# A log-sum-exp kernel on one core: whole loads until two tiles before the end, stores in rows of unequal counts, the last batch written in four parts

## The chip, the cores and the metric

The kernel runs on one core of a Trainium2 chip. The metric is device time in microseconds (us), lower is better. The profile's span is about 1.9 us shorter than that time (339.2 against 341.11 in the profiled run before), because it counts from the first to the last instruction.

The five engines are TensorE (PE), VectorE (DVE), ScalarE (ACT), GpSimd (POOL) and SyncE (SP), which here only issues DMAs. Sixteen DMA engines move the data.

## The reference

```python
B, S, D, H = 8, 2048, 2048, 8        # x: B x S x D, bias: H x 256, all float32
x_heads = x.reshape(B, S, H, 256).transpose(0, 2, 1, 3) + bias[None, :, None, :]
x_tiled = np.repeat(x_heads, 2, axis=2)
out = log(sum(exp(x_tiled)))         # over the last axis, with the usual maximum
```

134 MB are read and 1 MB is written. Each of the 16,384 rows of x gives eight sums of 256 exponentials, and each logarithm is written twice side by side.

## The kernel before

There are 64 tiles of 256 rows (2 MB: 128 partitions, two rows of 8 KB each). Tiles are counted from 0 to 63. In each tile TensorE adds the bias of heads 0 and 1 into PSUM, and ScalarE takes their exponentials with the sum; for the other six heads ScalarE takes exponentials in place and VectorE multiplies by exp(bias) and sums (twelve multiply-and-sum instructions a tile). Eight tiles make a batch; two tiles later its sums are transposed, ScalarE takes the logarithm, and 128 KB are stored. The parts that matter:

```python
NBUF = 9                                  # buffers of one tile
LAST_CUTS = [[0, 1024, 2048], [0, 512, 1024, 1536, 1792, 2048]]
def pieces(t):                            # how the load and the work of tile t are cut
    left = T - 1 - t
    if left > 8:
        return [(0, K, 0, D)]             # whole, K = 2 rows a partition
    if left > 3:
        return [(k, k + 1, 0, D) for k in range(K)]          # halves: tiles 55 to 59
    cuts = [[0, D // 2, D]] * K if left else LAST_CUTS       # quarters: 60 to 62
    ...
def finish(b, src, n_blk, k_rows, base, i, engines):
    ...                                   # transpose, logarithm (ScalarE) into res[i]
    parts = [(0, H)] if n_blk * n in (n, 2 * S) else [(h, h + 1) for h in range(H)]
    ...                                   # one store of 64 rows of 2 KB for a whole batch
for t in range(T):
    ...                                   # the work of tile t, piece by piece
    if t + NBUF < T:
        load(t + NBUF)
    fb, at = divmod(t - 2, NBLK)
    if fb >= 0 and at == NBLK - 1:
        finish(fb, ..., [nc.sync])        # batches 0 to 6, two tiles late
for k in range(K):                        # tile 63 by itself; tiles 56 to 62 were finished
    finish(B - 1, lambda _: Rz[:, k], 1, 1, S - (K - k) * P, k, [nc.sync])   # within it
```

The softmax here doesn't subtract the row's maximum and nothing guards it: scores larger than these inputs give would overflow.

## Time and profile before

The time before is 341.08 us (median of 3, 340.43 to 341.75). The page of the profile, cut. The two rows of slices cut the span in 40: the busy share of the DMA engines in tenths, and the rate in GB/s. The line below them is the share of the chain of waits by engine.

```profile
span 339.2 us, 3449 instructions
PE 238.3 (70%) x408; PEld 70.3 (21%) x408; DVE 271.8 (80%) x1538; ACT 295.0 (87%) x609; POOL 6.3 (2%) x14
...
DMA  8999999999999999999999999999999999988950
GB/s 300 427 433 428 424 429 430 429 429 426 425 430 430 423 427 424 436 423 428 425 435 417 431 425 428 430 428 425 429 432 424 428 418 420 422 346 277 309 209 19
...
q14 instruction: 20, 0.16, 0.1%
...
DMA 75%; ACT 17%; PE 4%; POOL 1%; issue 1%; DVE 0%; POOLq 0%; DVEq 0%; SPq 0%; ACTq 0%
```

ScalarE is busy for 87%, but the chain is DMA for 75%. The chain in order of time shows why: start, duration, what. A tile costs ScalarE 4.44 us (from one exponential of a whole tile, 2.65 us, to the next) as long as data lies ready. Then it has caught up, and the chain jumps to loads.

```profile
20.81 2.65 ACT xt L164
23.46 0.40 ACT ps L156 x2
23.88 0.87 ACT ps L156 x4
24.77 0.47 ACT ps L156 x2
25.25 2.65 ACT xt L164
...
58.93 35.23 DMA xt<-in_x_dram
```

SyncE's timeline (start, duration, what, count; a row covers all issues of a kind in a row) shows one store a batch, and the waits of its queue (total us, times, longest us) show what it waits for. In this kernel a DMA is issued only when the DMA eight before it has landed (the first line), so eight are in flight; a load also waits until VectorE has freed its buffer (the second).

```profile
58.93 4.76 SPq L90 DMA_DIRECT2D xt<-in_x_dram  x2
63.89 0.55 SPq L214 DMA_DIRECT2D out_dram<-res  x1
68.81 32.94 SPq L90 DMA_DIRECT2D xt<-in_x_dram  x8
105.27 0.47 SPq L214 DMA_DIRECT2D out_dram<-res  x1
```

```profile
SPq L90 <- DMA xt<-in_x_dram: 153.3, 59, 5.4
SPq L90 <- DVE R L170: 111.5, 51, 7.5
SPq L214 <- DMA xt<-in_x_dram: 16.5, 7, 3.5
```

The fall of the rate at the end of the page, from 422 to 277 GB/s, looks like bandwidth that small packets lose. It is not. The trace also records when each of the sixteen DMA engines marks a DMA as done. Counted from it, this is how far the others are ahead of the last one:

```
load (from 1)  landed (last mark)   second-last engine ahead by   first engine ahead by
     4             23.31                     0.2 us                     1.0 us
    24            124.78                     2.0 us                     4.3 us
    44            227.46                     5.7 us                     8.3 us
    55            283.58                     7.0 us                    10.3 us
```

One engine falls behind. It takes 4.89 us for its share of a load, like the others, but about every 25.7 us a load takes it 5.86 us. At each of those steps an 8 KB packet of instruction fetch (queue 14 of the page) lies in the trace: it takes 0.325 us, and the 16 KB packet after it 1.273 us in place of 0.61 us, 0.98 us together, close to the step of 0.97 us. (The packets carry no engine's number; that these fetches run on the late engine is what run e7 below shows.) At 300 us the other engines have run out of issued work, which thins the rate; the late one goes on at full speed. A load counts as landed only when the late one is done, so **the late engine's sum of work sets the time**. After the last landing (331.62 us) come another 7.57 us of arithmetic and stores.

The last lines of ScalarE before; "L199" is a logarithm, a bracket is idle time and its releaser:

```profile
332.72 0.58 ACT L199 ACTIVATE res<-tps 56x512 f32<-56x512 f32 x1
333.20 1.75 ACT L164 ACTIVATE xt<-xt 128x512 f32<-128x512 f32 x4
334.85 0.36 ACT L199 ACTIVATE res<-tps 8x256 f32<-8x256 f32 x1
336.48 0.37 ACT L199 ACTIVATE res<-tps 8x256 f32<-8x256 f32 x1 [1.28 <-PE tps L186]
```

ScalarE ends its last exponential at 334.95, 3.3 us after the last landing: at the end the arithmetic lags behind the loads.

### The profile page before, as it was taken

What the parts mean: (1) busy time and instruction counts of PE and PEld (TensorE: products, weight loads), DVE (VectorE), ACT (ScalarE), POOL (GpSimd) and SP (SyncE); (2) the same over time, 40 slices, a digit from 0 to 9 for tenths busy, and PEclk for the clock granted to TensorE, in tenths of its full rate; (3) what the DMA queues carried; (4) which work ended last, traced back from release to release, by engine and by line L of the source; (5) the groups of instructions that cost most, each with busy time, mean ns of one, the idle gap of its engine ahead of it and who ended that gap; (6) DMA issues with size and microseconds to landing.
All of it is one profiled execution on the core that took longest, in us unless ns stands there. A gap on an engine that the chain in (4) does not pass through costs nothing.

```text
span 339.2 us, 3449 instructions
## 1 busy us (share of the span) xinstructions
PE 238.3 (70%) x408; PEld 70.3 (21%) x408; DVE 271.8 (80%) x1538; ACT 295.0 (87%) x609; POOL 6.3 (2%) x14
## 2 busy tenths in 40 slices
PE   5296985866785966776965765766766667868791
PEld 2031222221121221221221221221221212212120
DVE  0429999998887887887898798797798788998775
ACT  2379999998997997988998898898899899998895
POOL 6100000000000000000000000000000000000000
PEclk9999577587876587876589877698777698595756
DMA  8999999999999999999999999999999999988950
GB/s 300 427 433 428 424 429 430 429 429 426 425 430 430 423 427 424 436 423 428 425 435 417 431 425 428 430 428 425 429 432 424 428 418 420 422 346 277 309 209 19
DMA packets 12921, 135.50 MB, mean 399 GB/s; under 512 B 1625, under 2 KB 1897, under 8 KB 4577
## 3 DMA queue, kind: packets, MB, share of 16 engines
q1 hardware_dynamic: 12800, 135.27, 95.6%
q14 instruction: 20, 0.16, 0.1%
q8 instruction: 3, 0.05, 0.1%
q10 hardware_dynamic: 2, 0.01, 0.0%
q0 software_dynamic: 96, 0.00, 0.0%
HBM read 134.23 MB, written 1.05 MB: 399 GB/s over the span
## 4 chain that ended last, share of the span: by engine, by line
DMA 75%; ACT 17%; PE 4%; POOL 1%; issue 1%; DVE 0%; POOLq 0%; DVEq 0%; SPq 0%; ACTq 0%
DMA xt<-in_x_dram 72%; ACT xt L164 10%; ACT ps L156 6%; PE ps L150 3%; DMA b<-bparts 2%; DMA brow<-in_bias_dram 1%; PE ps L145 1%; ACT res L199 0%; DVE junk L170 0%; POOL brest L117 0%; POOL brest L119 0%; POOL bparts L116 0%; POOL bparts L118 0%; POOL b L122 0%; POOL bparts L120 0%
## 5 line engine op out<-in xcount | busy, mean ns | idle before, releaser
L170 DVE CUSTOM_DVE_ANT_0 junk<-xt,w_rep 128x256 f32<-128x256 f32 x768 | 271.0, 420 | 63.4 <-ACT xt L164 63.2
L150 PE MATMUL ps<-xt,ident 128*128 128x512 f32 x256 | 188.8, 872 | 84.0 <-DMA xt<-in_x_dram 83.5
L164 ACT ACTIVATE xt<-xt 128x3072 f32<-128x3072 f32 (+4 forms) x83 | 179.4, 2172 | 20.0 <-DMA xt<-in_x_dram 17.2
L156 ACT ACTIVATE ps<-ps 128x256 f32<-128x256 f32 x256 | 94.6, 370 | 14.0 <-PE ps L150 9.2
L150 PEld LDWEIGHTS ps<-xt,ident 128*128 128x128 f32 x256 | 58.0, 254 | 164.5 <-DMA xt<-in_x_dram 119.5
L170 DVE DVE_READ_ACCUMULATOR2_ANT R<- 128x1 f32 x756 | 61.9, 82 | 0.0
L145 PE MATMUL ps<-b,ones 3*128 3x512 bf16 x128 | 47.0, 439 | 6.5 <-DMA b<-bparts 6.5
L156 ACT ACTIVATION_READ_ACCUMULATOR ps<-ps 128x1 f32 x256 | 48.7, 190 | 0.0
L145 PEld LDWEIGHTS <-ones 3*128 3x128 bf16 x128 | 7.9, 95 | 83.1 <-issue 75.1
L126 PE MATMUL ps<-brow,ones 1*128 1x512 f32 x6 | 5.5, 1078 | 3.6 <-DMA brow<-in_bias_dram 3.6
L133 ACT ACTIVATE w_rep<-ps 128x512 f32<-128x512 f32 x3 | 1.8, 597 | 5.9 <-PE ps L126 5.9
L199 ACT ACTIVATE res<-tps 64x512 f32<-64x512 f32 (+2 forms) x10 | 5.3, 535 | 1.3 <-PE tps L186 1.3
L186 PEld LDWEIGHTS tps<-ident,R 128*64 128x64 f32 (+1 forms) x16 | 2.4, 150 | 7.9 <-ACT ps L156 5.0
L186 PE MATMUL tps<-ident,Rz 128*8 128x128 f32 x2 | 0.7, 374 | 4.1 <-DVE Rz L170 4.1
L186 PE MATMUL tps<-ident,R 128*64 128x128 f32 (+1 forms) x16 | 3.6, 317 | 0.0
L126 PEld LDWEIGHTS ps<-brow,ones 1*128 1x128 f32 x6 | 1.8, 323 | 5.6 <-issue 5.6
L100 ACT ACT_TABLE_LOAD x1 | 1.3, 1283 | 0.7 <-PEq L279 0.7
L122 POOL DMA_DIRECT2D b<-bparts x3 | 1.6, 540 | 0.0
L117 POOL TENSOR_TENSOR brest<-brow,bparts 1x512 f32<-1x512 f32 x1 | 1.1, 1143 | 0.1
L119 POOL TENSOR_TENSOR brest<-brest,bparts 1x512 f32<-1x512 f32 x1 | 1.1, 1142 | 0.1
L186 PEld LDWEIGHTS tps<-ident,Rz 128*8 128x8 f32 x2 | 0.2, 83 | 4.7 <-DVE Rz L170 2.4
L170 DVE DVE_READ_ACCUMULATOR2_ANT Rz<- 128x1 f32 x12 | 1.0, 83 | 0.0
(11 smaller groups left out, 3.0 us busy)
## 6 DMA issues: line engine op xcount, KB each, us to landing
xt<-in_x_dram SPq DMA_DIRECT2D x55, 2048.0 KB
xt<-in_x_dram SPq DMA_DIRECT2D x10, 1024.0 KB
xt<-in_x_dram SPq DMA_DIRECT2D x14, 512.0 KB
out_dram<-res SPq DMA_DIRECT2D x7, 128.0 KB
xt<-in_x_dram SPq DMA_DIRECT2D x3, 256.0 KB
xt<-in_x_dram SPq DMA_DIRECT2D x2, 128.0 KB
out_dram<-res SPq DMA_DIRECT2D x8, 14.0 KB
b<-bparts POOLq DMA_DIRECT2D x3, 1.0 KB, 5.6
```

Source lines behind the costliest of these rows:

```text
L100: nc.scalar.add_instruction(mybir.InstLoadActFuncSet(name=nc.get_next_instruction_name(), act_func_set_id=set_idx,))
L117: nc.gpsimd.tensor_sub(brest[:, 0], bp, bparts[:, 0])
L122: nc.gpsimd.dma_start(out=b3[i : i + 1, :], in_=bparts[:, i])
L126: nc.tensor.matmul(ps[i], lhsT=ones, rhs=brow[:, CPE + c : CPE + c + MM], start=True, stop=True,)
L133: nc.scalar.activation(out=w_rep[:, c : c + MM], in_=ps[i], func=ACT.Exp)
L145: nc.tensor.matmul(p[:, 0:CPE], lhsT=ones3, rhs=b3, start=True, stop=False)
L150: nc.tensor.matmul(p[:, 0:CPE], lhsT=ident, rhs=v, start=False, stop=True)
L156: nc.scalar.activation(out=p[:, c : c + Dh], in_=p[:, c : c + Dh], func=ACT.Exp, accum_out=dst(h),)
L164: nc.scalar.activation(out=v, in_=v, func=ACT.Exp)
L170: nc.vector.tensor_tensor_reduce(out=j, in0=v, in1=w_rep[:, c : c + Dh], scale=1.0, scalar=0.0, op0=ALU.mult, op1=ALU.add, accum_out=dst,)
L186: nc.tensor.transpose(out=tps[i][0:nr, k], in_=src(k), identity=ident)
L199: nc.scalar.activation(out=rv, in_=tv, func=ACT.Ln)
```

## The change

The intent, as far as the code tells it: larger packets near the end; less store work for the high-numbered DMA engines; and the last batch's bulk written early and from another queue, so that SyncE is free for the last stores. The diff, cut to its core:

```diff
+STORE_ROWS = [
+    [15, 14, 13, 12, 10], [11, 9, 16, 16, 12], [16, 16, 16, 8, 8],
+    [16, 16, 16, 9, 7], [16, 16, 16, 10, 6], [16, 16, 16, 11, 5], [16, 16, 16, 12, 4],
+]                                   # (line breaks changed here)
 ...
-        if left > 8:
+        if left > 1:
             return [(0, K, 0, D)]
-        if left > 3:
-            return [(k, k + 1, 0, D) for k in range(K)]
-        cuts = [[0, D // 2, D]] * K if left else LAST_CUTS
+        cuts = [[0, D]] * K if left else LAST_CUTS
 ...
-        parts = [(0, H)] if n_blk * n in (n, 2 * S) else [(h, h + 1) for h in range(H)]
+        if n_blk == 1:
+            step, parts = 2 * S, [H]
+        elif n_blk == NBLK:
+            step, parts = n, STORE_ROWS[b]      # five stores a batch
+        else:
+            step, parts = n, [n_blk] * H        # last batch: eight stores of 6 rows
 ...
         for k0, k1, c0, c1 in pieces(t):
+            if left == 0 and c1 == D and k0 > 0:
+                finish(B - 1, lambda k: Rz[:, k0 - 1], ...)   # first half of tile 63
 ...
+            if left == 0 and c0 == 0:
+                if k0 == 0:
+                    finish_batch(B - 1, nc.gpsimd)            # tiles 56 to 61
+                elif k0 == 1:
+                    finish(B - 1, lambda k: Ry[:, k], ...)    # tile 62
 ...
-    for k in range(K):
-        finish(B - 1, lambda _: Rz[:, k], 1, 1, S - (K - k) * P, k, [nc.sync])
+    finish(B - 1, lambda _: Rz[:, K - 1], 1, 1, S - P, 1, nc.sync)
```

More of the change, by code (lines that the diff above doesn't have):

```diff
@@ L22 @@
 LAST_CUTS = [[0, 1024, 2048], [0, 512, 1024, 1536, 1792, 2048]]
+STORE_ROWS = [
+    [15, 14, 13, 12, 10],
+    [11, 9, 16, 16, 12],
+    [16, 16, 16, 8, 8],
+    [16, 16, 16, 9, 7],
+    [16, 16, 16, 10, 6],
+    [16, 16, 16, 11, 5],
+    [16, 16, 16, 12, 4],
+]
 @with_exitstack
@@ L57 @@
     brest = sb.tile([1, 2, CPE], F32, name="brest")
-    nblk = [NBLK] * (B - 1) + [NBLK - 1]
+    nblk = [NBLK] * (B - 1) + [NBLK - 2]
     R = [sb.tile([P, K, H, nblk[b]], F32, name=f"R{b}") for b in range(B)]
+    Ry = sb.tile([P, K, H], F32, name="Ry")
     Rz = sb.tile([P, K, H], F32, name="Rz")
@@ L179, in weigh, with finish @@
         )
-    def finish(b, src, n_blk, k_rows, base, i, engines):
+    def finish(b, src, n_blk, k_rows, base, i, engine):
         nr = H * n_blk
@@ L199, in finish @@
         nc.scalar.activation(out=rv, in_=tv, func=ACT.Ln)
-        parts = [(0, H)] if n_blk * n in (n, 2 * S) else [(h, h + 1) for h in range(H)]
-        for q, (h0, h1) in enumerate(parts):
-            rows = (h1 - h0) * n_blk
+        if n_blk == 1:
[4 more added lines that the diff above has]
+            step, parts = n, [n_blk] * H
+        r0 = 0
+        for rows in parts:
+            h, m = divmod(r0, n_blk)
             ov = bass.AP(
                 tensor=out.tensor,
-                offset=out.offset + (b * H + h0) * 2 * S + 2 * base,
-                ap=[[n if n_blk > 1 else 2 * S, rows], [1, n]],
+                offset=out.offset + (b * H + h) * 2 * S + 2 * base + m * n,
+                ap=[[step, rows], [1, n]],
             )
@@ L210, in finish, with finish_batch @@
                 tensor=rs.tensor,
-                offset=rs.offset + h0 * n_blk * rs.ap[0][0],
+                offset=rs.offset + r0 * rs.ap[0][0],
                 ap=[[rs.ap[0][0], rows], [1, n]],
             )
-            engines[q % len(engines)].dma_start(out=ov, in_=iv)
+            engine.dma_start(out=ov, in_=iv)
+            r0 += rows
+        assert r0 == nr
+    def finish_batch(b, engine):
+        finish(
+            b,
+            lambda k: R[b][:, k].rearrange("p h n -> p (h n)"),
+            nblk[b],
+            K,
+            0,
+            b % 2,
+            engine,
+        )
     for t in range(T):
@@ L219 @@
         xt = xts[t % NBUF]
-        last = t == T - 1
+        left = T - 1 - t
         def sum_at(k, h):
-            return Rz[:, k, h : h + 1] if last else R[b][:, k, h, blk : blk + 1]
+            if left > 1:
+                return R[b][:, k, h, blk : blk + 1]
+            return (Ry if left else Rz)[:, k, h : h + 1]
         for k0, k1, c0, c1 in pieces(t):
+            if left == 0 and c1 == D and k0 > 0:
+                finish(
+                    B - 1,
+                    lambda k: Rz[:, k0 - 1],
+                    1,
+                    1,
+                    S - (K - k0 + 1) * P,
+                    0,
+                    nc.sync,
+                )
             if c0 == 0:
@@ L236 @@
                     weigh(xt[:, k, c : c + Dh], c // Dh, sum_at(k, c // Dh))
-            if last and k0 == K - 1 and c0 == 0:
-                finish(
-                    b,
-                    lambda k: R[b][:, k].rearrange("p h n -> p (h n)"),
-                    NBLK - 1,
-                    K,
-                    0,
-                    1,
-                    [nc.sync],
-                )
+            if left == 0 and c0 == 0:
+                if k0 == 0:
+                    finish_batch(B - 1, nc.gpsimd)
+                elif k0 == 1:
+                    finish(B - 1, lambda k: Ry[:, k], 1, K, S - 2 * K * P, 0, nc.sync)
         if t + NBUF < T:
@@ L251 @@
         if fb >= 0 and at == NBLK - 1:
-            finish(
-                fb,
-                lambda k: R[fb][:, k].rearrange("p h n -> p (h n)"),
-                NBLK,
-                K,
-                0,
-                fb % 2,
-                [nc.sync],
-            )
-    for k in range(K):
-        finish(B - 1, lambda _: Rz[:, k], 1, 1, S - (K - k) * P, k, [nc.sync])
+            finish_batch(fb, nc.sync)
+    finish(B - 1, lambda _: Rz[:, K - 1], 1, 1, S - P, 1, nc.sync)
     order.__exit__(None, None, None)
```

## The prediction

> **What bounds the kernel now.** DMA, and within it one of the sixteen DMA engines. The chain of waits is 72% loads of xt. In the timeline of SyncE every DMA first waits for the landing of the DMA eight before it, so eight are in flight. From 60 to 300 us a 2 MB load lands every 4.89 us (428 GB/s), while ScalarE needs 4.44 us a tile (chain, 20 to 55 us), so ScalarE, though 87% busy, follows. The sixteen completion marks of each load, which the trace records, show that all engines but one finish a load 7 to 11 us ahead of the last one by 300 us: that one loses 0.97 us every 25 us, each time an 8 KB instruction-fetch packet runs on it. So the fall to 269 GB/s near 310 us is not lost bandwidth; the other engines have run out of work and the late one still runs at full rate. Its sum of work is the kernel's time, plus 7.6 us from the last landing (331.6) to the end (339.2).
>
> **What the change takes away (late engine).** A tile of 16 KB packets lands in 4.89 us, in 8 KB packets 4.96, in 4 KB packets 5.01. Whole loads for tiles 55 to 61 and halves for 62 save about 5x0.07 + 2x0.12 + 0.05 = 0.64 us. A store of a batch costs it 0.33 us (four 2 KB packets of 84 ns); six of them precede the last load. The Trainium skill (DMA: Bandwidth & Descriptors, "Why a DMA increments its semaphore by 16 and not by 1") says that a DMA's rows are spread over the largest k up to 16 that divides them, on the lowest-numbered k engines; the trace agrees in number: 64 rows leave 16 marks, 7 rows leave 7 and one of the issuer. So the unequal row counts load the low-numbered engines. If the late one is the highest, it carries 14 rows in place of 24: 0.8 us saved (estimate). If it is a middle one, about 0.2 us is lost. The trace doesn't tell which it is.
>
> **What it adds.** (1) Five stores a batch take five of the eight places in flight, so only three loads stay queued; at 4.89 us each that still covers the late engine: no cost. (2) Tile 61 becomes usable only when whole. From then ScalarE has tile 61 (4.5 us), two halves of 62 (2.4 each), tile 63 in pieces (4.8), and three logarithms before the last (1.3), against landings that end 10 us after tile 61's. I sum its last logarithm to about 17.5 us after that landing, 1.5 to 2.5 us later than now at equal landings (now the last exponential ends 3.3 us after the last landing). TensorE at half clock (2.6 us a half tile) can add one more. (3) Eight stores through GpSimd: at the start such a store took 0.54 us to issue and 5.6 us to land. Issued around 332 us, the last can land near 341, later than SyncE's last.
>
> **Sum.** Minus 0.4 to 1.4, plus 1.5 to 2.5, plus 0 to 2: 341.8 us, 8 in 10 between 338.8 and 344.8. Chances: faster 0.03, within 2% 0.94, slower 0.03.
>
> **What would show it.** Landings of loads still 4.89 us apart; last load landing 0.4 to 1.4 us earlier; the stretch from last landing to end grown from 7.6 to 9 to 11 us; ScalarE without idle time in it; the share of small packets down. GpSimd's issues on the chain at the end if (3) binds.
>
> **What would make it wrong.** The late engine gaining more, or another becoming last; three queued loads not being enough; GpSimd's stores landing in 2 us, or much later; TensorE's clock in the last 20 us.

## The result, and the profile after

After: 343.22 us (median of 4, 342.79 to 343.46). Before, with a fourth run: 340.79 us (340.43 to 341.75). The ratio is 1.0065, 95% interval 1.0041 to 1.009. A ratio here is the mean time of one kernel's fast runs over that of the other's of the same rounds, so not quite the ratio of the medians quoted. In a later group of runs (after2, below) the same kernel gave 343.03 against 341.22, ratio 1.0051 (1.0039 to 1.0063). So by the medians the change costs 1.8 to 2.4 us.

The page after, the same lines:

```profile
span 341.4 us, 3425 instructions
PE 235.2 (69%) x410; PEld 69.7 (20%) x410; DVE 271.6 (80%) x1538; ACT 295.2 (86%) x597; POOL 10.4 (3%) x22
...
GB/s 302 430 430 429 427 430 427 426 425 426 424 429 429 430 429 419 431 426 429 430 424 425 428 428 427 379 402 428 430 419 389 397 428 429 396 380 397 366 57 16
...
q14 instruction: 20, 0.16, 0.1%
```

The busy times of VectorE and ScalarE are the same to a part in a thousand. The rate falls later at the end, but dips now also at the 26th and 27th and at the 31st and 32nd slice (379 to 402 GB/s). SyncE's timeline shows what else is new:

```profile
58.74 4.77 SPq L100 DMA_DIRECT2D xt<-in_x_dram  x2
64.17 20.79 SPq L230 DMA_DIRECT2D out_dram<-res  x5
89.64 12.65 SPq L100 DMA_DIRECT2D xt<-in_x_dram  x8
105.68 19.84 SPq L230 DMA_DIRECT2D out_dram<-res  x5
131.50 12.18 SPq L100 DMA_DIRECT2D xt<-in_x_dram  x8
```

```profile
SPq L230 <- DMA xt<-in_x_dram: 131.5, 36, 5.5
```

For some 25 us no load is issued (from 64.17 to 89.64), since each of the five stores waits for the load eight places before it (the last line: 131.5 us of such waits, where the stores before had 16.5); then loads follow in a bunch. And the end of ScalarE; below it GpSimd's stores, from the timeline and from the list of issues (KB each, median us from issue to landing):

```profile
334.68 0.57 ACT L209 ACTIVATE res<-tps 8x512 f32<-8x512 f32 x1
335.16 1.44 ACT L174 ACTIVATE xt<-xt 128x512 f32<-128x512 f32 x3
337.03 0.37 ACT L209 ACTIVATE res<-tps 8x256 f32<-8x256 f32 x1 [0.43 <-DMA out_dram<-res]
337.31 0.40 ACT L174 ACTIVATE xt<-xt 128x256 f32<-128x256 f32 x1
338.64 0.37 ACT L209 ACTIVATE res<-tps 8x256 f32<-8x256 f32 x1 [0.94 <-PE tps L196]
```

```profile
333.23 3.97 POOL L230 DMA_DIRECT2D out_dram<-res  x8 [324.11 <-ACT res L209]
...
out_dram<-res POOLq DMA_DIRECT2D x8, 12.0 KB, 1.7
```

The last exponential (337.31) now stands behind the logarithm of the first half of tile 63, which had to wait. Before, it ended at 334.95; now at 337.71. The bracket names what that logarithm waited for: a store, that of tile 62's results (issued at 335.28, landed at 336.94), which leaves the same buffer, `res[0]`. Its own sums were ready, their transpose had ended at 335.91. One more result buffer would take this wait away; no run tried that. The eight stores of GpSimd are issued in 3.97 us and landed 1.7 us later in the median (the last at 338.44, where SyncE's last landed at 340.33): they are not what ends last.

The last load landed at 331.46 us, hardly earlier than before (331.62). From there to the end it takes 9.89 us in place of 7.57. That comparison misleads: the profiled run of before happens to have one more step of 0.93 us in its landings, at 320.23 us. The chain of before goes through that landing and then through TensorE (L145 and L150 add the bias), at a granted clock (the share of its full speed that TensorE gets) of 0.50 to 0.51 from 320 to 330 us:

```profile
307.18 13.05 DMA xt<-in_x_dram
320.23 0.04 issue
320.27 2.07 PE ps L150 x2
322.35 0.53 PE ps L145
```

So the table below cuts at the 60th landing of a whole tile, ahead of that. The stretch from the 16th to the 60th landing shows the late engine; the stretch from there to the end of the span shows the rest. Both are counted from one profile each. The second also holds chances of the one execution: e1_rows and e9_four16, which end as before does but for the stores of batch 6, have 29.78 and 29.18 there without the extra step; and from 320 to 325 us TensorE's granted clock was 0.50 in before, after and after2 but 0.66 and 0.68 in e2 and e5. Half a microsecond in that column decides nothing.

```
run          edit                                       16th to 60th   60th to end   span
before                                                     225.31         29.50      339.2
after        all                                           225.97         30.71      341.4
after2       all, once more                                226.46         30.66      341.4
e1_rows      unequal rows alone                            226.17         29.78      340.5
e2_pieces    new pieces alone                              224.88         30.23      339.7
e3_last      last batch alone                              225.23         29.65      339.3
e4_rz0_end   after, one logarithm moved back               226.20         30.42      340.9
e5_equal     after with 64-row stores                      224.85         30.69      340.1
e6_defer     before, stores held back                      223.53         28.89      337.0
e9_four16    before, 4 stores of 16 rows                   225.53         29.18      339.3
e10_60_4     before, stores of 60 and 4 rows               225.71         29.86      340.2
e11_best     e6 with whole loads to tile 59                223.15         29.06      336.6
```

### The profile page after: what moved, and what is told of

It reads as the page before. It is cut to its first block, busy times and chain, and to the rows that moved or that the text cites. A ratio compares the mean times of both kernels' runs of the same rounds, so it can differ in the third digit from the quotient of the medians.

```text
span 341.4 us, 3425 instructions
## 1 busy us (share of the span) xinstructions
PE 235.2 (69%) x410; PEld 69.7 (20%) x410; DVE 271.6 (80%) x1538; ACT 295.2 (86%) x597; POOL 10.4 (3%) x22
## 5 line engine op out<-in xcount | busy, mean ns | idle before, releaser
L160 PE MATMUL ps<-xt,ident 128*128 128x512 f32 x256 | 184.3, 859 | 88.6 <-DMA xt<-in_x_dram 88.3
L174 ACT ACTIVATE xt<-xt 128x3072 f32<-128x3072 f32 (+3 forms) x70 | 177.7, 2541 | 24.5 <-DMA xt<-in_x_dram 19.9
L230 POOL DMA_DIRECT2D out_dram<-res x8 | 4.0, 505 | 324.1 <-ACT res L209 324.1
L209 ACT ACTIVATE res<-tps 64x512 f32<-64x512 f32 (+3 forms) x11 | 5.9, 540 | 1.4 <-PE tps L196 0.9
L196 PE MATMUL tps<-ident,R 128*64 128x128 f32 (+1 forms) x16 | 4.3, 363 | 0.0
```

The lines of the kernel that those rows point to most:

```text
L160: nc.tensor.matmul(p[:, 0:CPE], lhsT=ident, rhs=v, start=False, stop=True)
L174: nc.scalar.activation(out=v, in_=v, func=ACT.Exp)
L196: nc.tensor.transpose(out=tps[i][0:nr, k], in_=src(k), identity=ident)
L209: nc.scalar.activation(out=rv, in_=tv, func=ACT.Ln)
L230: engine.dma_start(out=ov, in_=iv)
```

## The experiments

Each kernel had five timed rounds and one profile; runs of one group ran on one chip. All results were correct.

### First group: the three parts one by one

**e1_rows**: before, with batches 0 to 6 stored by STORE_ROWS.

```diff
+        if n_blk == NBLK:
+            for rows in STORE_ROWS[b]:
+                ...  # as in the change
+            return
```

> The kernel before with only the unequal row counts. Theory: the late DMA engine is one of the four lowest-numbered (in the trace of after, even the stores of 4 and 5 rows finish last on it), so it gets 5 rows a batch in place of 4: each batch's store costs it 0.41 us in place of 0.31, six batches come before the last load, so the last load lands about 0.6 us later and the time rises by 0.3 to 0.8 us. Rival (what the row counts seem to be made for): the late engine is a high-numbered one and is relieved, the time falls by about 0.8 us. Second rival: five stores take the places of loads in flight and starve the queue: then several us slower.

Measured: 342.05 against 341.41 us, ratio 1.0019 (0.9999 to 1.004). It is slower, not faster, though the interval touches 1. The landings are clearer: 0.86 us more between the 16th and the 60th. The rival that wanted relief for a high-numbered engine falls.

**e2_pieces**: before, with only the new `pieces`.

```diff
-        if left > 8:
+        if left > 1:
             return [(0, K, 0, D)]
-        if left > 3:
-            return [(k, k + 1, 0, D) for k in range(K)]
-        cuts = [[0, D // 2, D]] * K if left else LAST_CUTS
+        cuts = [[0, D]] * K if left else LAST_CUTS
```

> The kernel before with only the new pieces (tiles up to 61 whole, 62 in halves). Theory: the last load lands 0.4 to 0.7 us earlier, but ScalarE gets tile 61 only when it is whole and ends 1.5 to 2 us later behind the last landing: together 0.8 to 1.5 us slower than before. Rival: larger packets are a plain gain, 0.6 us faster.

Measured: 341.41 against 341.41, ratio 0.9998 (0.998 to 1.0016). Neither theory's number came: I had expected 0.8 to 1.5 us slower. The table has both halves of the theory at a smaller size: 0.43 us gained up to the 60th landing, 0.73 us lost behind it (one profile each; the extra step and the clock in before make the second uncertain). The timed runs say zero: what is gained is not left at the end.

**e3_last**: after, with the old pieces and one 64-row store a batch, that is, before with the last batch in four parts.

```diff
-STORE_ROWS = [ ... ]
+STORE_ROWS = [[64]] * 7
 ... (and pieces as in before)
```

> The kernel before with only the last batch in four parts, the first through GpSimd; old pieces, 64-row stores. Theory: landings unchanged; ScalarE has one logarithm more (0.57 us) and, ahead of the last exponential, the logarithm of the first half of tile 63, for which it idles 0.4 us: 0.7 to 1.4 us slower than before. Rival: taking eight stores off SyncE's queue lets the last stores go earlier: 0.3 to 0.8 us faster.

Measured: 341.31 against 341.41, ratio 1.0005 (0.9982 to 1.0029). No change; the expected 0.7 to 1.4 us did not come with the old pieces. Why not is not shown.

**e4_rz0_end**: after, with the finish of the first half of tile 63 behind the last exponential.

```diff
-            if left == 0 and c1 == D and k0 > 0:
-                finish(B - 1, lambda k: Rz[:, k0 - 1], ...)
 ...
-    finish(B - 1, lambda _: Rz[:, K - 1], 1, 1, S - P, 1, nc.sync)
+    for k in range(K):
+        finish(B - 1, lambda _: Rz[:, k], 1, 1, S - (K - k) * P, k, nc.sync)
```

> The kernel after with the logarithm and store of the first half of tile 63 put back behind the last exponential, as in before. Theory: the last exponential no longer waits behind it (0.43 us idle and 0.36 us of work): 0.4 to 0.8 us faster than after, about 1.6 to 2.0 us slower than before. Rival: the backlog of tile 61 alone sets the end and the place of that logarithm doesn't matter: same as after, 2.4 us slower than before.

Measured: 342.68 against 341.41, ratio 1.0042 (1.0021 to 1.0062). After itself was not in this group; in the next one it stood 1.81 us above before, so by the medians the place of that logarithm costs about 0.5 us (1.81 less 1.27), across two chips. The two intervals overlap, and the profiles say 0.2 to 0.3 us (30.42 against 30.71 and 30.66 from the 60th landing on), so it is not clear of the noise. ScalarE's end shows the idle time gone:

```profile
334.97 1.74 ACT L174 ACTIVATE xt<-xt 128x512 f32<-128x512 f32 x4
336.81 0.37 ACT L209 ACTIVATE res<-tps 8x256 f32<-8x256 f32 x1
```

Alone, the parts cost 0.64, 0.00 and -0.10 us by the medians, 0.5 us together. All at once they cost 1.8 to 2.4 us. That suggests that something interacts, and the next group looks for it; but the intervals of the three reach 0.6 to 0.8 us to either side, so the sum does not show it.

### Second group: what interacts, and whether one DMA engine is the bound

**after2**: after, unchanged, on the chip of this group.

> The kernel after, unchanged, so that the other runs have it on the same chip. Both theories: 2.0 to 2.6 us slower than before.

Measured: 343.03 against 341.22, ratio 1.0051 (1.0039 to 1.0063). 1.81 us slower, less than I had expected.

**e5_equal**: after, with 64-row stores.

```diff
-STORE_ROWS = [ ... ]
+STORE_ROWS = [[64]] * 7
```

> The kernel after with 64-row stores of batches 0 to 6 as in before (new pieces and new last batch kept). Theory: the parts add up unlike alone: the rows cost 0.6 us, and pieces and last batch, each about free when alone, cost 1.3 to 1.8 us together, because the pieces use up the slack of ScalarE at the end and the two extra waits of the last batch then have none: 0.4 to 0.8 us faster than after. Rival: the unequal rows are what interacts (they thin out the loads in flight just where whole tiles need them): then this one is as fast as before, 2 us faster than after.

Measured: 341.70 against 341.22, ratio 1.0013 (1.0001 to 1.0025); 1.33 us faster than after on the same chip. This lies between the two theories. The unequal rows are the larger part of the loss: 1.33 of 1.81 us, against 0.48 for pieces and last batch together. In the landings the rows cost 1.1 to 1.6 us beside the new pieces, after 0.86 us alone: e5 needs 224.85 us between the 16th and the 60th landing, after 225.97 and 226.46. But three profiles with the same rows and pieces (after, e4, after2) scatter by 0.5 us, and the interval of e1, 0.0 to 1.4 us, holds 1.33: that the rows cost more in company than alone is not shown.

**e6_defer**: before, with the results of batches 0 to 5 kept and stored behind the last load.

```diff
-    res = [sb.tile([H * NBLK, P, K, 2], F32, name=f"res{i}") for i in range(2)]
+    res = [sb.tile([H * NBLK, P, K, 2], F32, name=f"res{i}") for i in range(B)]
+    resz = [sb.tile([H, P, 2], F32, name=f"resz{i}") for i in range(2)]
+    held = []
 ...
-        rs = res[i]
+        rs = res[b] if n_blk > 1 else resz[i]
 ...
-            engines[q % len(engines)].dma_start(out=ov, in_=iv)
+            if b < B - 2:
+                held.append((ov, iv))
+            else:
+                engines[q % len(engines)].dma_start(out=ov, in_=iv)
 ...
             load(t + NBUF)
+        if t + NBUF == T - 1:
+            for ov, iv in held:
+                nc.sync.dma_start(out=ov, in_=iv)
```

> The kernel before, with the results of batches 0 to 5 kept in their own tiles and stored after the last load has been issued. Theory (the late DMA engine is what everything waits for, and each batch's store costs it 0.31 us ahead of the loads): the last load lands 1.5 to 2.0 us earlier and the time falls by 1.2 to 2.0 us. Rival (the bytes of the stores don't matter, DMA is at its common limit and moves the same bytes in all): no change, or slower as the stores pile up at the end.

Measured: 339.00 against 341.22, ratio 0.9935 (0.9916 to 0.9954): 2.2 us faster with the same bytes moved, a little more than expected. The rival falls. The stores now sit at the end of SyncE's queue, where the late engine works them off (the last of them is marked at 332.39) while ScalarE finishes:

```profile
300.87 22.52 SPq L92 DMA_DIRECT2D xt<-in_x_dram  x15
324.30 4.90 SPq L256 DMA_DIRECT2D out_dram<-res  x6
329.29 4.64 SPq L219 DMA_DIRECT2D out_dram<-res  x9
```

The landings differ from those of before by one step of 0.3 us each batch: 0.24 us at the 16th, then -0.04, -0.35, -0.60, -0.89, -1.21 at the 20th, 28th, 36th, 44th and 52nd.

**e7_more_dve**: before, with six tiny VectorE instructions more in each of the first 56 tiles.

```diff
+            if t < 56:
+                for _ in range(6):
+                    nc.vector.memset(scratch, 0.0)
```

> The kernel before with six more one-column VectorE instructions in each of the first 56 tiles (336 instructions[...]: two to three fetch packets of 8 KB more). Theory (the late DMA engine is the one that also fetches VectorE's instructions, 0.97 us a fetch): two or three more steps of 0.97 us in the landings, 1.9 to 2.9 us slower, though VectorE gets idle time enough to hold them. Rival (the late engine is late for some other reason): less than 0.5 us slower.

Measured: 343.96 against 341.22, ratio 1.0078 (1.0065 to 1.009), 2.7 us slower. The page, which counts the fetches of all engines, has two packets more, and VectorE still idles for 15% of the span:

```profile
span 342.2 us, 3791 instructions
...
q14 instruction: 22, 0.18, 0.1%
```

The steps in the landings show it best. Before, landings with a step stand at 79.47, 105.20, 130.67, 156.40 and 187.04 us: mostly 25.7 us apart. Here they stand at 74.64, 95.20, 116.05, 136.59 and 157.44: 20.7 us apart, each 0.97 us as before. VectorE has 30 instructions a tile in place of 24, and 25.7 us times 24/30 is 20.6. Up to the 60th landing there are 13 such steps in place of 10, and that landing comes 2.91 us later, three steps. So the late DMA engine is the one that fetches VectorE's instructions, and this kernel, bound by loads, pays for them. (The profiled run had a granted TensorE clock of 0.55; the other five had 0.73 to 0.79 and the same times within 1.0 us, so the clock is not the cause.)

### Third group: the fifth row or the fuller queue, and a better kernel

**e9_four16**: before, each batch in four stores of 16 rows: as many rows for each engine as before, but four places in the queue.

```diff
+            for rows in [16, 16, 16, 16]:
```

> The kernel before with each batch's store as four DMAs of 16 rows: every engine still gets 4 rows, only the number of DMAs grows, so fewer loads stay in flight. Theory A (the cost of the unequal rows is the fifth row on the late engine): same as before, within 0.3 us. Theory B (the cost is the thinning of the queue: the other engines run dry and come back all at once, which slows the late one): 0.3 to 0.8 us slower, with landings of more than 4.95 us after the batches.

Measured: 342.10 against 341.41, ratio 1.0022 (1.0001 to 1.0043). The landings drift by only 0.06 us up to the 56th and by 0.22 us up to the 60th. The runs fall into two groups, 341.18 and 341.23, and four from 342.06 to 342.30. By its median this leans to theory B, but weakly: before fell into two groups here as well (340.08 to 340.70 and 341.41 to 341.92), and the profiled run of e9 is one of the two fast ones (341.18), so its landings cannot show what the other four lost.

**e10_60_4**: before, stores of 60 and 4 rows, so that the four lowest-numbered engines get a fifth row at the cost of one more place.

```diff
+            for rows in ([60, 4] if b < 6 else [48, 10, 3, 2, 1]):
```

> The kernel before with the stores of batches 0 to 5 as 60 rows and 4 rows: engines 0 to 3 get 5 rows, the last one none, and only two DMAs take places in flight. Batch 6, behind the loads, is stored as 48, 10, 3, 2 and 1 rows so that the last marks show which engine is the late one. Theory A (the fifth row): each batch drifts the landings by 0.10 us, 0.5 to 0.7 us slower than before. Theory B (thinning alone): same as before within 0.3 us. If the late engine is number 0, the mark of the one-row store comes 0.18 us after the two-row one's; if it is 1, 2 or 3, the stores of fewer rows than that come early.

Measured: 341.56 against 341.41, ratio 1.0011 (0.9988 to 1.0034); in two groups again (340.59 to 341.05, and 342.06 to 342.13). By time nothing is settled. The landings show the fifth row: 0.09, 0.07, 0.07, 0.08 and 0.05 us a batch, 0.40 us up to the 60th. The marks of batch 6 tell which engine is late:

```
store of batch 6   issued    last mark
48 rows            327.10    332.32    behind the last load (332.09)
10 rows            328.29    332.49    also behind it
 3 rows            329.49    330.70    1.2 us after its issue, ahead of it
 2 rows            330.12    331.32
 1 row             330.77    331.90
```

A store of 4 rows (batch 0) was marked last at 99.79, right behind the late engine's 60-row share at 99.60. So the late engine takes part in a store of four rows and not in one of three. Counted from 0, by the rule that the prediction cites (the rows go to the lowest-numbered engines), it is engine 3; the number rests on that rule. The change gave it five rows in every batch (four in none), the opposite of relief.

**e11_best**: e6_defer, with whole loads up to tile 59.

```diff
-        if left > 8:
-            return [(0, K, 0, D)]
         if left > 3:
-            return [(k, k + 1, 0, D) for k in range(K)]
+            return [(0, K, 0, D)]
```

> The kernel before with the stores of batches 0 to 5 held back until the last load is issued, and whole loads up to tile 59 (60 to 62 in quarters, 63 as before). Theory: 2.2 us for the stores, and 0.35 us for the larger packets, which here cost ScalarE nothing because tiles 60 to 62 still come in quarters: 2.2 to 2.7 us faster than before, 0.99 of it. Rival: packet size gives nothing back, as with the pieces alone: 2.2 us.

Measured: 339.20 against 341.41, ratio 0.9945 (0.9924 to 0.9966). Its landings gain 0.38 us over e6 (up to the 60th, one profile each), but the time does not: the two are the same within their intervals. Either beats both kernels; e6_defer is the smaller edit.

## Why the prediction was right or wrong

The predicted time was 341.8 us, with 338.8 to 344.8 as the range; 343.22 came, within 2% of before as foreseen. Foreseen was a loss of 0.7 us (341.8 against 341.08), and 1.8 to 2.4 came. That the time still fell into the range is in part luck: the range is 6 us wide, and two terms were wrong in opposite directions. Of the signs that it named, the long stretch behind the last landing came (9.89 us); a last landing 0.4 to 1.4 us earlier (it was 0.16) and a ScalarE without idle time did not.

- **The bound: right.** One late DMA engine sets the landings. e6 (taking stores off its way, 2.2 us faster with the same bytes) and e7 (more instruction fetch, 2.7 us slower) show it; e10 and the rule of the prediction make it engine 3.
- **"If it is a middle one, about 0.2 us is lost": mis-sized, and the failed step of the sum.** The case that came had no number in it: one of the four lowest-numbered engines, with five rows in every batch, for which six packets of 84 ns would have made 0.5 us. The unequal rows cost 0.64 us alone (0.0 to 1.4) and 1.33 us within the change. The fifth row accounts for about 0.08 us a batch, 0.4 to 0.5 us in six batches (e10).
- **"Three loads stay queued; that still covers the late engine: no cost": doubtful.** In the two profiles of after the landings lose 1.1 to 1.6 us against e5 between the 16th and the 60th, two to four times what the fifth row explains. In the profile of after, the landing behind each batch's stores comes 0.10 to 0.15 us later than in e5, 0.7 us in six batches, and the 59th landing alone adds 0.43. In after2 the 52nd, 53rd and 59th add most: the 52nd load lands 4.97 us after the last store's mark and the 53rd 5.10 us after the 52nd, where the same two steps in after are 4.35 and 4.90. Theory B of e9 would have the other engines, all starting again at once, slow the late one. But in both profiles six loads had been issued in a bunch (within 3.6 us from 264.08 in after2, 2.5 us from 264.53 in after), and only one shows the delay there; and e9 shows it only weakly. This part of the loss is measured, and its mechanism is open.
- **Packets: right in mechanism, too large in size.** 0.64 us was predicted for all pieces; 0.43 to 0.46 us came up to the 60th landing (e2, e5). e2's time shows that none of it is left at the end.
- **"1.5 to 2.5 us later than now at equal landings": too large.** From the last landing the end grew by 2.3 us (7.57 to 9.89), but the extra step in the profiled run of before made its last landing, and so its 7.57, not comparable. From the 60th landing to the end, new pieces and last batch cost 1.2 us (29.50 to 30.69, e5), of which the pieces alone make 0.7 (e2); the extra step and TensorE's clock make these uncertain by half a microsecond or more. By time, the two parts together cost 0.48 us (e5) with their gain in the landings of 0.46 counted in. From 0.2 to 0.5 us comes from the logarithm put ahead of the last exponential (e4, not clear of the noise). That order I had counted only as its work of 0.37 us; its wait of 0.43 us for the buffer I had not.
- **GpSimd, "0 to 2": zero.** Its stores landed 1.7 us after issue, behind the last load; I had taken 5.6 us from small copies at the start of the kernel, where loads were in flight. That the loads make this difference is likely, and no run tests it. The Trainium skill (DMA: Bandwidth & Descriptors, "Anatomy of one DMA — SWDGE (gpsimd) path") gives about 2.0 us as the fixed cost of such a DMA, which is near the 1.7 here and does not cover the 5.6 at the start.

So the term for the rows was too small by one to two microseconds, and that for the end, with GpSimd's, too large by about as much.

## What to carry to other kernels

When a kernel waits for loads, ask which of the sixteen DMA engines finishes last before changing packet sizes: a load lands with its slowest engine, and small traffic ahead of the loads costs full time on that one (here 0.3 us a store and 0.97 us an instruction fetch). Put stores that nobody waits for behind the last load, where arithmetic hides them. Near the end of a kernel, keep engines that work in order from waiting: here an exponential that was ready stood behind a logarithm that waited 0.43 us for its result buffer.

## What the Trainium skill lacked or had wrong

- Instruction fetch (Runtime: NRT & Kernel Launch, "Instruction fetch mechanics") is called mostly hidden there, in blocks of 16 KiB. Here VectorE's fetches show as 8 KB packets about every 25.7 us, and each holds up data of the same DMA engine for about 0.98 us, 0.325 us for itself and 0.66 us in the next packet; in this kernel, bound by loads, this is not hidden (e7: 2.7 us for three fetches more). No page tells this cost.
- On a slow DMA engine, DMA: Bandwidth & Descriptors ("Latency and other measured facts") names engines 7 and 15 as usually slower, and calls that specific to SWDGE. Here, with loads from SyncE, the late one is engine 3 (by the rule of the next point), up to 10 us behind the first, for the reason above.
- The rule for the number of engines (the same page, "Why a DMA increments its semaphore by 16 and not by 1") held in every store looked at: 64 rows gave 16 marks, 10 rows 10 and 3 rows 3, each of the last two with one more of the issuer. That it is the lowest-numbered engines that take part no run here shows: the marks carry no numbers.
- That page ("Rules for kernel authors") advises against many small transfers for their overhead. No page says that each also takes one of the places in flight: here SyncE issued no load for some 25 us while five stores waited in line. How much of the 1.3 us that the five stores cost is due to this stays open.
- No page has the two groups of times about 1 us apart that e9 (341.2 and 342.2) and e10 (340.9 and 342.1) show, and before in the same group less clearly; the distance is near that of one fetch step. The profiles of e10 (a run of its slower group) and e9 (of its faster) differ by 0.7 us behind the 60th landing (29.86 against 29.18); the cause stays open.
